# Some of the second weight parts made by GpSimd instead of VectorE, in two stretches of a two-block transformer kernel

## The chip, the cores and the metric

One core of one Trainium2 chip runs the whole program in one launch. The metric is the device time of one execution in microseconds (us), the lower the better; the median of several runs counts. The engines are named as the profile names them: PE (TensorE, matmuls; PEld is its weight load), DVE (VectorE), ACT (ScalarE), POOL (GpSimd), SP (the queue that issues the weight transfers).

## The reference, cut to what matters

Two transformer blocks follow each other on 256 tokens of width 1024, all in fp32. Block 1 has a mixer (an mLSTM of four heads beside a sliding-window attention of eight heads), a cross attention to 256 memory rows, and PEER: product keys choose 16 of 16384 experts for each token and head, of which each is one row of `expert_down` and one of `expert_up`. Block 2 has gated linear attention (GLA) beside MoBA attention, an MLP with squared ReLU, and a gated embedding. Shortened:

```
proj = rmsnorm(h, g_mix) @ w_in            # mq mk mv mo gates aq ak av
h = h + concat([mlstm(...), window(...)]) @ w_out
h = h + cross_attention(rmsnorm(h), rmsnorm(mem), ...)
h = h + peer_ffn(rmsnorm(h), ...)          # then a final norm
u = rms_norm(x, norm_mix_2) @ w_in_2       # gq gk gv lr gr mq mk mv gates
x = x + (sigmoid(ga)*gla(...) + sigmoid(gb)*moba(...)) @ w_out_2
x = x + square(relu(rms_norm(x) @ w_up_2)) @ w_down_2 ; x = x + gate*(p @ w_ple_2)
```

Every product of a weight with an activation is a dense matmul; PEER is computed over all experts with a gate that is zero for those not chosen.

## The kernel before, in words

Matmuls run in a rounded fp32 format, and each fp32 operand is split in two parts to keep its precision: `hi` is the value rounded, `lo` is the value less `hi`. A product is three matmuls: hi by hi, hi by lo, lo by hi (`mm3`, L339 to L341, where the weight is the stationary operand, and L378 to L380 in `unit_N`, where the activation is).

Weights come in 494 chunks of 128 x 1024 fp32 (512 KB), in the order of the list `ORDER`. The class `Stream` carries each through the same steps: SP issues the transfer into one of four `raw` tiles; ACT casts it to `hi` (L123, one of four tiles); DVE or POOL subtracts to get `lo` (L135, one of four tiles); PE uses both. `Stream.take(name)` is called by PE's code for each chunk c. It first issues the cast for all chunks up to c + 3 and the subtraction for all up to c + 2. Which engine subtracts is read from `PLAN`, a table from a chunk's name to a pattern that holds from that chunk on; the entry of the pattern is the chunk's number modulo the pattern's length. `AV` means cast on ACT and subtraction on DVE, `AG` means cast on ACT and subtraction on POOL:

```
self.pattern = self.plan.get(self.order[c][0], self.pattern)
first, second = self.pattern[c % len(self.pattern)]
...
(self.nc.vector if eng == "V" else self.nc.gpsimd).tensor_tensor(lo[:, o], raw[:, o], hi[:, o],
                                                                op=OP.subtract)
```

Everything else is written as chains: Python generators (`Chains`) that issue a few instructions at each tick. A tick comes after each unit of matmuls. So the order of the instructions of each engine is fixed when the program is built: it is the order in which takes, evacuations and ticks issue them, and each engine runs its own in that order.

The mixers' middle has the chunks mk0, mk1, mq0, mq1, mo0 to mo3 (numbers 11 to 18). Around them lie the chains `mem_chain` (splits and squares the memory: DVE L305, POOL adds L462 and L464), `mlstm` (a scan at L511, exponents from PSUM at L525 and L527, a POOL triangle mask at L532), the convolution in the evacuation of mk and mq (`ev_conv`, DVE L682 to L686), and `window` (DVE L636 to L642). The chunk after them is xk0.

Block 2 begins with bk0 to bk7, bq0 to bq7, lr0, gv4 to gv7 (numbers 331 to 351), each unit of four chunks in `unit_N`. The chain `norms` runs beside them: it adds up squares of the residual, on DVE (L1033, L1099) and POOL (L1034, L1100), sums them over partitions on PE (L1105), and gets 1/sqrt by `newton` (L286 to L300) on two numbers per partition, in some ten small DVE instructions. Evacuations of the units of block 2 are held until `norms` is done, as they need its scale: bk's are ACT L1388 and, per head, DVE L1286 (squares and their sum). Units of `unit_N` use two of five PSUM banks. The chain `setup` (POOL memsets L1273 to L1275), `keys` (L1256, L1262), `queries` and `stream` follow. The chunk after gv7 is gk0.

Of the kernel before, what the change touches and what calls it, by code (L numbers as in the profile page):

```python
# [52 lines left out]
for _name, _w in (("avg", 3), ("aq", 4), ("mk", 2), ("mq", 2), ("mv", 4), ("mo", 4), ("xk", 8), ("xv", 8),  # L53
# [18 lines left out]
          ("keys", 0): 1, ("keys", 1): 1, ("keys", 2): 3, ("keys", 3): 1, ("keys", 4): 2, ("queries", 1): 3,  # L72
          ("gla", 1): 1, ("gla", 8): 1, ("gla_out", 2): 1}

PLAN = {"mv0": ("AV",), "xo2": ("AG",), "down20": ("AV",), "down28": ("AG",), "down45": ("AV",),
        "upw0": ("AV", "AG"), "upw122": ("AV",), "up3": ("AV", "AG"), "up31": ("AV",)}


def chunks(s):
# [129 lines left out]
def block_kernel(ctx, tc, xT, memT, pT, wst, dwn, upw, keysT, gate_w2, cols, rows, out):  # L209
# [20 lines left out]

    ws.plan = PLAN
    ch = Chains()
# [1393 lines left out]
```

## Time and profile before

| | |
|---|---|
| time, median of 3 runs | 1566.12 us (1564.64 to 1566.81) |
| the profiled execution, its own time | 1564.55 us |
| its span, first to last instruction | 1562.8 us |
| busy: PE, PEld | 98%, 91% |
| busy: DVE, ACT, POOL | 73%, 51%, 27% |
| DMA | 169 GB/s read from HBM over the span |

The span is 1.75 us shorter than the execution's own time. Times in rows are us from the span's start. A row of the timeline gives start, duration, engine, line, operation, tiles and shapes, how many instructions are merged in it, and in brackets how long the engine had been idle before and what ended that.

### The profile page before, as it was taken

The numbers are of one execution on the slowest core, as the hardware profiler recorded it, in microseconds if no ns is written. First come the engines' busy times: TensorE is split into PE (matmuls) and PEld (weight loads), VectorE is DVE, ScalarE is ACT, GpSimd is POOL, SyncE is SP. The second block draws the span as 40 slices with busy tenths as digits, with TensorE's granted clock in tenths as the row PEclk, the third lists the DMA queues.
The fourth block names the chain that finished last, engine by engine and source line by source line (L and its number), as shares of the span: only waits on it lengthen the run. The fifth ranks groups of instructions, "written<-read, shape, count | busy, mean of one in ns | idle before, by whom it ended". The sixth has DMA issues, their size and how long they took to land.

```text
span 1562.8 us, 27506 instructions
## 1 busy us (share of the span) xinstructions
PE 1528.3 (98%) x10818; PEld 1417.9 (91%) x10818; DVE 1145.2 (73%) x2070; ACT 800.9 (51%) x1338; POOL 425.8 (27%) x238
## 2 busy tenths in 40 slices
PE   9899999999999999999999999999999999999998
PEld 8799999999999999998888888877888999999998
DVE  7977753877978899967777777759984656876456
ACT  7655553554445555454554554546654644544443
POOL 2210077645400000014444444403030000386000
PEclk9999999999999999999999999999999999999999
DMA  8335455455454444455656666645454365566553
GB/s 273 112 109 172 144 161 164 147 166 174 150 184 152 156 156 155 156 178 192 196 189 192 198 192 195 193 152 181 145 180 153 111 189 176 162 189 210 188 178 120
DMA packets 75713, 265.32 MB, mean 170 GB/s; under 512 B 8368, under 2 KB 11952, under 8 KB 75584
## 3 DMA queue, kind: packets, MB, share of 16 engines
q1 hardware_dynamic: 74848, 262.31, 52.9%
q8 instruction: 84, 1.38, 0.4%
q10 hardware_dynamic: 736, 1.27, 0.3%
q14 instruction: 45, 0.37, 0.1%
HBM read 262.49 MB, written 1.05 MB: 169 GB/s over the span
## 4 chain that ended last, share of the span: by engine, by line
PE 84%; DVE 13%; issue 1%; ACT 1%; DMA 1%; POOL 0%; SPq 0%; DVEq 0%; ACTq 0%; POOLq 0%
PE mm L339 16%; PE mm L341 16%; PE mm L340 16%; PE mm L1020 7%; PE mm L1018 7%; PE mm L1019 7%; DVE lo L135 3%; PE mm L380 2%; PE mm L379 2%; PE mm L378 2%; PE at L964 2%; DVE cb L877 1%; DVE cb L874 1%; DVE scr L1286 1%; DVE cb L876 1%
## 5 line engine op out<-in xcount | busy, mean ns | idle before, releaser
L123 ACT CAST hi<-raw 128x1024 fp32r<-128x1024 f32 (+1 forms) x495 | 517.0, 1046 | 290.1 <-issue 170.8
L135 POOL TENSOR_TENSOR lo<-raw,hi 128x1024 fp32r<-128x1024 f32 x134 | 325.3, 2428 | 738.6 <-ACT hi L123 736.5
L135 DVE TENSOR_TENSOR lo<-raw,hi 128x1024 fp32r<-128x1024 f32 (+1 forms) x361 | 447.7, 1250 | 25.4 <-ACT hi L123 25.1
L341 PE MATMUL mm<-XD,lo 128*128 128x256 f32 x1024 | 290.9, 284 | 6.7 <-DVE lo L135 6.7
L339 PE MATMUL mm<-XD,hi 128*128 128x256 f32 x1024 | 296.2, 289 | 0.0
L340 PE MATMUL mm<-XD,hi 128*128 128x256 f32 x1024 | 290.2, 283 | 0.0
L1003 DVE SCALAR_TENSOR_TENSOR ring<-cb,ring 128x256 fp32r<-128x256 f32 x128 | 172.0, 1345 | 94.0 <-ACT ring L1002 94.0
L341 PEld LDWEIGHTS mm<-XD,lo 128*128 128x128 f32 x1024 | 196.9, 192 | 7.9 <-DVE lo L135 7.9
L1018 PE MATMUL mm<-hi,ring 128*128 128x512 f32 x512 | 199.2, 389 | 1.0 <-DVE cb L984 1.0
L1020 PE MATMUL mm<-hi,ring 128*128 128x512 f32 x512 | 199.3, 389 | 0.0
L1019 PE MATMUL mm<-lo,ring 128*128 128x512 f32 x512 | 199.2, 389 | 0.0
L340 PEld LDWEIGHTS mm<-XD,hi 128*128 128x128 f32 x1024 | 197.1, 192 | 0.0
L339 PEld LDWEIGHTS mm<-XD,hi 128*128 128x128 f32 x1024 | 196.9, 192 | 0.0
L339 PE MATMUL mm<-XH,hi 128*128 128x256 f32 x584 | 168.6, 289 | 0.6 <-DVE hT L394 0.6
L341 PE MATMUL mm<-XH,lo 128*128 128x256 f32 x584 | 165.9, 284 | 0.6 <-DVE lo L135 0.6
L340 PE MATMUL mm<-XL,hi 128*128 128x256 f32 x584 | 165.8, 284 | 0.0
L1018 PEld LDWEIGHTS mm<-hi,ring 128*128 128x128 f32 x512 | 96.1, 188 | 21.0 <-ACT ring L1002 1.2
L339 PEld LDWEIGHTS mm<-XH,hi 128*128 128x128 f32 x584 | 112.6, 193 | 2.1 <-issue 1.5
L1020 PEld LDWEIGHTS mm<-hi,ring 128*128 128x128 f32 x512 | 96.1, 188 | 20.2 <-DVE ring L1003 0.4
L1019 PEld LDWEIGHTS mm<-lo,ring 128*128 128x128 f32 x512 | 96.1, 188 | 20.1
L341 PEld LDWEIGHTS mm<-XH,lo 128*128 128x128 f32 x584 | 112.6, 193 | 0.8 <-DVE lo L135 0.8
L340 PEld LDWEIGHTS mm<-XL,hi 128*128 128x128 f32 x584 | 112.6, 193 | 0.2
(464 smaller groups left out, 2963.5 us busy)
## 6 DMA issues: line engine op xcount, KB each, us to landing
raw<-in_wst SPq DMA_DIRECT2D x237, 512.0 KB, 3.7
raw<-in_dwn SPq DMA_DIRECT2D x128, 512.0 KB, 3.6
raw<-in_upw SPq DMA_DIRECT2D x128, 512.0 KB, 4.1
hT<-in_xT SPq DMA_DIRECT2D x4, 256.0 KB, 4.8
memt<-in_memT SPq DMA_DIRECT2D x1, 1024.0 KB, 6.1
out<-hT SPq DMA_DIRECT2D x7, 128.0 KB, 1.7
rowt<-in_rows ACTq DMA_DIRECT2D x1, 640.0 KB, 5.9
raw<-in_wst SPq DMA_DIRECT2D x2, 256.0 KB, 3.5
```

What stands on the lines that cost most here:

```text
L123: self.nc.scalar.copy(hi[:, o], raw[:, o])
L135: (self.nc.vector if eng == "V" else self.nc.gpsimd).tensor_tensor(lo[:, o], raw[:, o], hi[:, o], op=OP.subtract)
L339: T.matmul(ps, lhsT=wh, rhs=xh, start=start, stop=False)
L340: T.matmul(ps, lhsT=wh, rhs=xl, start=False, stop=False)
L341: T.matmul(ps, lhsT=wl, rhs=xh, start=False, stop=stop)
L378: T.matmul(pss[tb], lhsT=xh, rhs=h, start=kd == 0, stop=False)
L379: T.matmul(pss[tb], lhsT=xh, rhs=l, start=False, stop=False)
L380: T.matmul(pss[tb], lhsT=xl, rhs=h, start=False, stop=kd == 7)
L1003: V.scalar_tensor_tensor(lo, cb[:, j], 1.0 / GATE, hi, op0=OP.mult, op1=OP.subtract)
L1018: T.matmul(o, lhsT=ch, rhs=wh, start=j == 0, stop=False)
L1019: T.matmul(o, lhsT=ch, rhs=wl, start=False, stop=False)
L1020: T.matmul(o, lhsT=cl, rhs=wh, start=False, stop=j == 127)
```

## The change

Four entries are added to `PLAN`. The first pair makes the pattern ("AV", "AG") hold from mk0 up to xk0, the second from bk2 up to gk0.

```diff
-PLAN = {"mv0": ("AV",), "xo2": ("AG",), "down20": ("AV",), "down28": ("AG",), "down45": ("AV",),
-        "upw0": ("AV", "AG"), "upw122": ("AV",), "up3": ("AV", "AG"), "up31": ("AV",)}
+PLAN = {"mv0": ("AV",), "mk0": ("AV", "AG"), "xk0": ("AV",), "xo2": ("AG",), "down20": ("AV",), "down28": ("AG",), "down45": ("AV",),
+        "upw0": ("AV", "AG"), "upw122": ("AV",), "bk2": ("AV", "AG"), "gk0": ("AV",), "up3": ("AV", "AG"), "up31": ("AV",)}
```

By the chunk numbers the odd ones move: mk0, mq0, mo0, mo2 (11, 13, 15, 17) in the mixers, and bk2, bk4, bk6, bq0, bq2, bq4, bq6, lr0, gv5, gv7 (333 to 351) in block 2. For these 14 chunks the subtraction at L135 is issued on POOL instead of DVE, at the same place of the program; the casts, the transfers and the matmuls are issued as before.

## Rows read from the trace of the kernel before

**Rows 1.** Page, part 1: busy us, share of the span, instructions of each engine.
```profile
PE 1528.3 (98%) x10818; PEld 1417.9 (91%) x10818; DVE 1145.2 (73%) x2070; ACT 800.9 (51%) x1338; POOL 425.8 (27%) x238
```

**Rows 2.** Waits of PE, 28 to 77 us: total us, times, longest.
```profile
PE mm L379 <- DVE lo L135: 4.0, 4, 2.1
```

**Rows 3.** Waits of PE, 1049 to 1122 us.
```profile
PE mm L379 <- DVE lo L135: 2.5, 4, 0.8
```

**Rows 4.** Windows: stretch, length, busy us of each engine (instructions), clock, DMA.
```profile
45.00:60.00 15.00, 14.07 (x95) 11.82 (x94) 14.57 (x31) 6.00 (x7) 3.74 (x4) 1.00 0.27 95
60.00:77.00 17.00, 13.37 (x62) 9.69 (x62) 16.41 (x49) 13.90 (x29) 1.26 (x2) 1.00 0.41 116
...
1060.00:1078.00 18.00, 16.75 (x76) 13.48 (x77) 17.59 (x32) 12.62 (x20) 9.69 (x9) 1.00 0.52 176
1078.00:1100.00 22.00, 20.27 (x91) 15.96 (x90) 20.51 (x86) 9.12 (x12) 2.60 (x4) 1.00 0.56 178
```

**Rows 5.** Page, part 5: the subtraction on each engine, busy us, mean ns.
```profile
L135 POOL TENSOR_TENSOR lo<-raw,hi 128x1024 fp32r<-128x1024 f32 x134 | 325.3, 2428 | 738.6 <-ACT hi L123 736.5
L135 DVE TENSOR_TENSOR lo<-raw,hi 128x1024 fp32r<-128x1024 f32 (+1 forms) x361 | 447.7, 1250 | 25.4 <-ACT hi L123 25.1
```

**Rows 6.** Timeline of DVE in the expert-up stage.
```profile
1002.56 2.41 DVE L1003 SCALAR_TENSOR_TENSOR ring<-cb,ring 128x256 fp32r<-128x256 f32 x1 [1.03 <-ACT ring L1002]
1005.28 0.42 DVE L1003 SCALAR_TENSOR_TENSOR ring<-cb,ring 128x256 fp32r<-128x256 f32 x1 [0.31 <-ACT ring L1002]
```

**Rows 7.** Timeline of POOL, same stretch.
```profile
1002.30 2.40 POOL L135 TENSOR_TENSOR lo<-raw,hi 128x1024 fp32r<-128x1024 f32 x1 [3.04 <-ACT hi L123]
```

**Rows 8.** Timeline of ACT in the mixers: the cast of mk0.
```profile
32.72 1.03 ACT L123 CAST hi<-raw 128x1024 fp32r<-128x1024 f32 x1
```

**Rows 9.** Timeline of DVE in the mixers.
```profile
34.75 0.88 DVE L305 SCALAR_TENSOR_TENSOR meml<-memt,colt,memh 128x256 fp32r<-128x256 f32 x2 [0.27 <-ACT memh L304]
...
43.62 0.92 DVE L684 TENSOR_SCALAR m<-n,colt 128x256 f32<-128x256 f32 x1
44.58 1.53 DVE L686 SCALAR_TENSOR_TENSOR m<-n,colt,m 128x256 f32<-128x256 f32 x3
...
58.10 0.55 DVE L636 SCALAR_TENSOR_TENSOR sA<-at,maskA 128x384 f32<-128x384 f32 x1
```

**Rows 10.** Timeline of POOL in the mixers.
```profile
42.33 2.06 POOL L462 TENSOR_TENSOR memt<-memt 128x512 f32<-128x512 f32 x1 [0.74 <-ACT memt L460]
48.83 1.73 POOL L462 TENSOR_TENSOR memt<-memt 128x512 f32<-128x512 f32 x1 [4.44 <-ACT memt L460]
```

**Rows 11.** Timeline of POOL at the start of block 2.
```profile
1064.07 5.51 POOL L1034 TENSOR_TENSOR cb<-cb 128x512 f32<-128x512 f32 x3 [43.05 <-ACT cb L1096]
1069.66 1.60 POOL L1100 TENSOR_TENSOR cb<-cb 128x256 f32<-128x256 f32 x1
1072.16 0.95 POOL L1273 MEMSET rst<- 128x1024 f32 x1 [0.90 <-POOL cb L1100]
```

**Rows 12.** Timeline of DVE at the start of block 2.
```profile
1066.11 6.24 DVE L135 TENSOR_TENSOR lo<-raw,hi 128x1024 fp32r<-128x1024 f32 x3
...
1073.17 1.02 DVE L288 TENSOR_SCALAR rr<-nwi 128x2 int32<-128x2 int32 x1
```

**Rows 13.** Timeline of PE: bk6's second matmul, and bq0 going on after a wait.
```profile
1068.50 0.47 PE L379 MATMUL mm<-lo,XH 128*128 128x512 f32 x1
...
1076.66 0.50 PE L378 MATMUL mm<-hi,XH 128*128 128x512 f32 x1 [1.04 <-ACT kn L1388]
```

**Rows 14.** Timeline of DVE before the product keys, beside POOL's parts.
```profile
232.11 2.23 DVE L286 TENSOR_SCALAR nwi<-nwm 128x2 int32<-128x2 int32 x1
```

**Rows 15.** Timeline of PE, same place.
```profile
240.52 0.87 PE L321 MATMUL at<-cb,ones 128*128 128x128 f32 x4 [2.78 <-DVE cb L334]
```

**Rows 16.** Windows, columns as in rows 4: a stretch of low clock.
```profile
240.95:244.34 3.39, 3.39 (x18) 3.39 (x17) 1.42 (x4) 1.32 (x2) 1.52 (x1) 0.50 0.29 112
```

**Rows 17.** Groups of DVE instructions, 1078 to 1100 us, columns as in rows 5.
```profile
L1286 DVE SCALAR_TENSOR_TENSOR scr<-kn 128x128 f32<-128x128 f32 x16 | 4.7, 292 | 0.7
```

## The prediction

> **What bounds the kernel now.** The page comes first: PE is busy for 98% of the span, DVE for 73%, POOL for 27% [rows 1]. PE waits for little on the whole, so the change can win only what PE waits for in its two stretches, and can lose as much as it makes PE wait. The list of PE's waits, cut to each stretch, says how much there is to win: in the mixers PE waits four times for a second part made by DVE, 4.0 us together, in block 2's start four times, 2.5 us [rows 2, 3]. The table of windows says why: DVE is busy 14.57 of 15 us and 16.41 of 17 in the mixers, 17.59 of 18 and 20.51 of 22 in block 2 [rows 4]. There DVE sets the pace, and PE waits at the chunks whose subtraction stands far back in DVE's queue. So the question is not whether POOL has time (it is busy 1 to 10 us in these windows) but whether DVE gets time back, and whether POOL delivers in time.
>
> **What a moved part costs.** The groups by line give 1.25 us for the subtraction on DVE and 2.43 on POOL [rows 5]. Fourteen are moved, so 14 x 1.25 = 17.5 us of DVE work go and 34 us of POOL work come. But the two engines do not run freely beside each other. Lay the timelines of both over each other in the expert-up stage: one L1003 takes 0.42 us with POOL idle, and 2.41 us when it begins 0.26 us after a POOL subtraction of 2.40; it ends 0.27 us after that one's end [rows 6, 7]. DVE, which runs its queue in order, stood still; in that stage every second L1003 does. A tiny L286 before the product keys stands 2.23 us in the same way [rows 14]. What stands is an instruction with two inputs in SBUF, or one that reads SBUF alone like L286, or L684 with 0.92 us beside a POOL add [rows 9, 10]. L636, which reads PSUM and one SBUF tile, takes 0.55 us [rows 9]; such ones and max-reductions I take to pass.
>
> So a moved part gives DVE 1.2 us and takes up to 2.4, by what stands at the head of DVE's queue while POOL works. Where the head is of the standing kind that is a loss of up to 2.4 - 1.2 = 1.2 us for each.
>
> **The mixers, four parts.** I follow DVE's queue with this rule. *mk0:* its cast ends at 33.75 [rows 8], so POOL works until 36.2; L305, at 34.75 the next with two inputs [rows 9], stands for 1.45 us. With 1.2 us gone behind it that is +0.2. *mq0:* POOL makes it behind its first add L462 and ahead of the one at 42.33 [rows 10], until about 44.5. L684 comes 1.2 us earlier and ends no earlier than now, at 44.54 [rows 9]; the add, moved behind the part, now falls on the first L686, 1.5 us. Together +1.4. *mo0:* it comes behind the add of 48.83 [rows 10], and a small add follows it: three POOL instructions in a row under the next convolution's L684 and L686, +2.3, less 1.2 is +1.1. *mo2:* it falls on L636 and reductions [rows 9], which pass: +0.3, less 1.2 is -0.9. The sum is 0.2 + 1.4 + 1.1 - 0.9 = +1.8 us on DVE. The longest of PE's waits, 2.1 us, is for mo3's part [rows 2], which DVE still makes behind all this, so PE ends the stretch 1.8 us later. Bounds: -4.0, all of PE's waits [rows 2], to 4 x 1.2 = +4.8.
>
> **Block 2, the order of POOL's queue.** This is the largest term, and it is not about DVE's load. POOL has work of its own here: three adds L1034 from 1064.07 to 1069.58 and one L1100 to 1071.26, the first of which waits for ACT's squares [rows 11]. They are issued at the tick behind bk3's matmuls. bk6's subtraction is issued by the take of bk4, right behind this tick; on DVE it is the first of the three at 1066.11 [rows 12], behind L1033 and L1099 of the same tick. On POOL it comes behind all four adds: it begins at 1071.3 and ends 2.4 us later, at 1073.7, or 1.1 us later still if DVE's part of bk7 gets in between. PE wants it at 1068.50 [rows 13], and behind this matmul stands everything that PE has to do: 5.2 to 6.3 us of new wait, of which I take 5.5. The lower bound has the adds undisturbed, 1.73 us each [rows 10] and half of that for L1100: 1070.1, and 1072.5 with the part, +4.0. bk2 and bk4 are made before the adds, while DVE waits for ACT and PE: 0. bq0's part, next on POOL, ends 2.4 us behind bk6's, two chunks ahead of its use: 0. A raw tile is held until its subtraction is done, so bk6's lateness also delays the transfer into its tile, which is bq2's; PE is as late by then.
>
> **Clock.** Behind a wait of 2.78 us before the product keys [rows 15] PE runs 3.4 us at a granted share of 0.50, its lower level of 1.2 GHz [rows 16]; the trace has two more such stretches ahead of its end. A wait of 5.5 us should bring one: half of 3.4, +1.7. Bounds 0 and two stretches, 3.4.
>
> **The scale of `norms`.** PE's L1105, behind bk6, releases `newton`, and bq0 cannot go on before bk's evacuation L1388 has the scale; PE already waits 1.04 us for it [rows 13]. bk6's delay moves this whole chain and costs nothing twice. New is that bq2's part, cast when bk6's matmuls are over, falls on `newton`: one stand of some 2.0 us, against 0.9 us now (L288, 1.02 us beside POOL's memsets [rows 11, 12]): +1.1. The memsets move behind bq2's part, onto the rest of `newton`; the rows show an instruction of one SBUF input standing beside them and none of two, so I add nothing. Bounds 0, and 3.1 if every step stands beside the memsets, 2.0 us.
>
> The Trainium skill ("SBUF — State Buffer", section "Who interferes with whom") says that a two-input VectorE instruction collides with a GpSimd instruction that reads SBUF, and not with one that only writes it. By this rule the memsets hold none of the two-input steps and the sum stays as below; without it the sum would be 2.0 us more. The row of L288 agrees as far as it goes.
>
> **Block 2, the busy stretch.** From 1078 to 1100 us DVE does little but L1286 (two SBUF inputs, 0.29 us each [rows 17]), scales of the same kind, and subtractions. bq4, bq6 and lr0 are made beside them; each takes 2.4 and gives 1.2: +3.6 us. Of this PE's freed wait at bq6, no more than 0.8 [rows 3], and a little room at bq7 take 0.9: +2.7. gv5 and gv7 cost DVE as much, but none of PE's waits for parts is there: 0. Bounds: -2.5, all of PE's waits [rows 3], to +3.6.
>
> **Sum.** 1.8 + 5.5 + 1.7 + 1.1 + 2.7 = 12.8 us. On the profiled execution's own time, 1564.55 us (span 1562.8), that gives 1577.4; the median of the runs, 1566.12, is 1.6 higher and gives 1578.9. I say 1578. Nothing later takes it back: PE is busy throughout, and its later waits are for other things.
>
> **Rivals.** (1) *The lateness of bk6 alone.* Enough of DVE's instructions pass that it loses nothing on balance: mixers 0, busy stretch 0, scale 0; 5.5 + 1.7 = 7.2, 1573. For it: L636 passes; against: L1003 and L286 stand for nearly all of a part. (2) *Faster.* POOL's parts cost DVE nothing, and PE's waits for parts vanish: -4.0 - 2.5 = -6.5, 1560. Its place is mo1, mo3, bq3 and bq5; it decides if DVE's two-input instructions keep their length beside POOL, and bk6's part is there before 1068.5. Against it: rows 6 and 11. (3) *Nothing.* A part is issued two chunks ahead of its use and is ready in time wherever it is made: 1566. Against it: PE waits for eight parts now. (4) *Worse.* Two stretches of slow clock and all terms at their upper bounds: 4.8 + 6.3 + 3.4 + 3.1 + 3.6 = 21.2, 1587.
>
> The Trainium skill ("Perfetto Trace Analysis", section "Optimizing Scalar/DVE Operations") says that with VectorE saturated, handing work to another engine, even GpSimd, may make sense, which would be rival 2, and adds that these two share a read port, so that it might not help. The rows of L1003 agree with the second half.
>
> **How the numbers follow.** The forecast (1574 to 1583) has 0.62, rival 1 (1569.5 to 1574) 0.15, worse (beyond 1583) 0.13, nothing 0.06, faster 0.04. A difference under 0.2%, 3.1 us, is about what a measurement of this kernel cannot tell from no change. Forecast, rival 1 and worse are slower by more: 0.90; same 0.06; faster 0.04. For 8 in 10 the range takes in the forecast, most of rival 1 and the lower part of worse: 1570 to 1585.
>
> **What would show it.** Right: bk6's part on POOL begins behind L1100, PE waits over 4 us for it at its second matmul, with a stretch at 0.50 behind; L684, L686 and L1286 stand for up to 2.4 us beside POOL's parts; PE's wait for mo3 is as long or longer. Wrong: bk6's part is there before PE wants it, or L1286 keeps 0.29 us while POOL subtracts. If POOL takes bk6's part ahead of the adds, the largest term is gone and the sign is open.

## The result, and the profile after

The changed kernel takes 1577.86 us (median of 4 runs, 1576.46 to 1579.96), beside 1566.13 for the kernel before on the same chip: 1.008 times as long, 95% interval 1.0064 to 1.0095, or 11.7 us. The forecast was 1578, 1570 to 1585, and slower.

The profiled execution took 1579.96 us (span 1578.3). Page, parts 1 and 5, as in [rows 1, 5]:

```profile
PE 1537.0 (97%) x10818; PEld 1424.8 (90%) x10818; DVE 1148.3 (73%) x2056; ACT 801.4 (51%) x1338; POOL 459.1 (29%) x252
...
L135 POOL TENSOR_TENSOR lo<-raw,hi 128x1024 fp32r<-128x1024 f32 x148 | 360.7, 2438 | 818.0 <-ACT hi L123 802.9
L135 DVE TENSOR_TENSOR lo<-raw,hi 128x1024 fp32r<-128x1024 f32 (+1 forms) x347 | 429.3, 1246 | 26.5 <-ACT hi L123 26.3
```

Read the first row against the third. DVE lost 14 subtractions and 18.4 us in the group of L135, yet its busy time did not fall: it rose by 3.1 us. The work went away and the time stayed, in other instructions that took longer.

PE's waits in block 2's start, 1049 to 1135 us (total us, times, longest), to set beside [rows 3]:

```profile
PE mm L379 <- POOL lo L135: 4.3, 1, 4.3
PE mm L378 <- ACT kn L1388: 3.5, 1, 3.5
PE mm L379 <- DVE lo L135: 2.3, 3, 1.2
PE at L321 <- DVE dg L1128: 1.5, 1, 1.5
```

The waits for DVE's second parts, which the change could have won, are as long as before (2.3 against 2.5 us). Two new ones stand above them: bk6's part on POOL, and the scale of `norms`, which was 1.04 us [rows 13]. The mixers, 28 to 80 us, to set beside [rows 2]:

```profile
PE at L632 <- DVE sA L636: 2.2, 1, 2.2
PE mm L379 <- DVE lo L135: 0.7, 2, 0.4
```

There the wait for mo3's part did shrink, from 2.1 to 0.3 us (the 0.4 is mo1's), and one of the size it had for `window`'s L636 came ahead of it.

Where bk6's part was, on POOL's timeline (compare [rows 11]):

```profile
1060.81 2.85 POOL L135 TENSOR_TENSOR lo<-raw,hi 128x1024 fp32r<-128x1024 f32 x1 [3.30 <-ACT hi L123]
1065.30 4.70 POOL L1034 TENSOR_TENSOR cb<-cb 128x512 f32<-128x512 f32 x3 [1.65 <-ACT cb L1096]
1070.08 0.79 POOL L1100 TENSOR_TENSOR cb<-cb 128x256 f32<-128x256 f32 x1
1070.83 5.65 POOL L135 TENSOR_TENSOR lo<-raw,hi 128x1024 fp32r<-128x1024 f32 x2
```

The first row is bk4's part. The last holds bk6's and bq0's: bk6's begins when L1100 ends. On PE's timeline bk6's first matmul, its second behind the wait, bk7's first, bq0 going on behind its wait, and bq1's first:

```profile
1069.51 0.39 PE L378 MATMUL mm<-hi,XH 128*128 128x512 f32 x1
...
1074.20 0.50 PE L379 MATMUL mm<-lo,XH 128*128 128x512 f32 x1 [4.30 <-POOL lo L135]
...
1079.23 0.48 PE L378 MATMUL mm<-hi,XH 128*128 128x512 f32 x1
...
1086.38 0.79 PE L378 MATMUL mm<-hi,XH 128*128 128x512 f32 x1 [3.46 <-ACT kn L1388]
...
1090.39 0.63 PE L378 MATMUL mm<-hi,XH 128*128 128x512 f32 x1
```

From such first matmuls comes the table that the experiments are read by. Each entry is the start of a chunk's first matmul less that of an earlier chunk's, in us; labels are those of the experiments below.

| PE's time between first matmuls of | before | after | e2 | e3 | e4 | e5 | e8 | e11 |
|---|---|---|---|---|---|---|---|---|
| bk6 and bk7 | 3.63 | 9.72 | 9.71 | 7.49 | 10.25 | 4.00 | 3.67 | 7.51 |
| bk7 and bq1 | 6.95 | 11.16 | 9.78 | 9.26 | 6.92 | 13.18 | 7.70 | 6.93 |
| bq1 and lr0 | 23.54 | 25.37 | 25.93 | 27.26 | 23.54 | 25.72 | 27.44 | 23.56 |
| lr0 and gv7 | 17.18 | 18.92 | 18.92 | 20.39 | 17.19 | 18.93 | 18.92 | 17.19 |

The loss of the profiled execution is 6.1 + 4.2 + 1.8 + 1.7 = 13.9 us here, and the mixers add 0.7 (PE begins xk0 1.4 us later than before, of which 0.66 stood ahead of them). With the 0.66 us by which the two traces already differ ahead of the mixers, this is the 15.4 us between the two profiled executions; the medians are 11.7 apart, so this execution is one of the longer ones.

What DVE did at bk4 and at the scale of `norms`:

```profile
1062.70 2.04 DVE L135 TENSOR_TENSOR lo<-raw,hi 128x1024 fp32r<-128x1024 f32 x1 [1.31 <-ACT hi L123]
1064.66 4.19 DVE L1033 TENSOR_TENSOR cb<-cb 128x512 f32<-128x512 f32 x3
...
1079.92 3.28 DVE L286 TENSOR_SCALAR nwi<-nwm 128x2 int32<-128x2 int32 x1
1082.22 0.98 DVE L287 TENSOR_SCALAR nwh<-nwm 128x2 f32<-128x2 f32 x1
1083.23 1.02 DVE L288 TENSOR_SCALAR rr<-nwi 128x2 int32<-128x2 int32 x1
```

bk5's part took 2.04 us instead of 1.2 beside bk4's on POOL, so L1033 came later and fell on POOL's adds: 4.19 us. L286, two numbers per partition, stood for 3.28: POOL's part of bq2 ran from 1079.88 to 1082.28 and a memset from 1082.22 to 1083.17. L287 ended in the same moment as L286, at 1083.20, so only L288 comes on top, with the 1.02 us that it took before [rows 12]. The groups of L1286, 1085 to 1110 us, as [rows 17]:

```profile
L1286 DVE SCALAR_TENSOR_TENSOR scr<-kn 128x128 f32<-128x128 f32 x16 | 6.7, 421 | 0.7
L1286 DVE SCALAR_TENSOR_TENSOR scr<-qn 128x128 f32<-128x128 f32 x8 | 4.4, 555 | 0.3
```

421 and 555 ns are means over instructions that passed in 0.29 us and a few that stood for a whole part: 16 x (0.421 - 0.292) = 2.1 us in the first group. DVE in the mixers (compare [rows 9]), each time with POOL's part in the same microseconds except the last:

```profile
43.45 1.96 DVE L684 TENSOR_SCALAR m<-n,colt 128x256 f32<-128x256 f32 x1
45.44 2.44 DVE L686 SCALAR_TENSOR_TENSOR m<-n,colt,m 128x256 f32<-128x256 f32 x3
...
52.51 3.90 DVE L686 SCALAR_TENSOR_TENSOR m<-n,colt,m 128x256 f32<-128x256 f32 x3
...
60.23 0.55 DVE L636 SCALAR_TENSOR_TENSOR sA<-at,maskA 128x384 f32<-128x384 f32 x1
```

Windows, columns as in [rows 4]: the mixers, block 2's start, and two stretches behind the two waits.

```profile
45.00:60.00 15.00, 13.66 (x98) 12.10 (x96) 14.61 (x26) 4.87 (x6) 7.26 (x7) 1.00 0.34 106
60.00:77.00 17.00, 15.43 (x58) 10.89 (x59) 16.41 (x50) 13.72 (x29) 3.12 (x3) 0.80 0.30 96
1060.00:1078.00 18.00, 12.89 (x50) 9.88 (x49) 10.54 (x8) 9.87 (x16) 13.79 (x7) 0.92 0.45 150
1078.00:1100.00 22.00, 18.54 (x73) 14.85 (x72) 19.44 (x67) 8.75 (x11) 8.72 (x6) 0.83 0.49 157
...
1075.04:1078.45 3.41, 3.41 (x11) 2.67 (x9) 0.00 (x0) 0.00 (x0) 1.44 (x1) 0.50 0.95 330
1085.28:1092.10 6.82, 5.72 (x14) 4.46 (x15) 6.12 (x36) 3.47 (x5) 0.30 (x1) 0.50 0.27 82
```

In the mixers DVE is as busy as it was (14.61 and 16.41 us, 14.57 and 16.41 before), with fewer subtractions in it. Behind each of the two long waits PE runs at 0.50, the lower level of 1.2 GHz. The second such stretch ends at 1092.10, after bq1's first matmul: half of the 1.71 us between them, some 0.9, is in the table's 1.8 us from bq1 to lr0. The 0.80 of the window from 60 to 77 us is a stretch at half clock too; e2's profile has one in the same place (63.38 to 66.79 us), though its mixers are those of before.

### The profile page after: what moved, and what is told of

Read it like the earlier page. It is cut to its first block, busy times and chain, and to the rows that moved or that the text cites. A ratio compares the mean times of both kernels' runs of the same rounds, so it can differ in the third digit from the quotient of the medians.

```text
span 1578.3 us, 27512 instructions
## 1 busy us (share of the span) xinstructions
PE 1537.0 (97%) x10818; PEld 1424.8 (90%) x10818; DVE 1148.3 (73%) x2056; ACT 801.4 (51%) x1338; POOL 459.1 (29%) x252
## 4 chain that ended last, share of the span: by engine, by line
PE 82%; DVE 13%; ACT 1%; issue 1%; DMA 1%; POOL 1%; SPq 0%; DVEq 0%; ACTq 0%; POOLq 0%
PE mm L339 16%; PE mm L341 16%; PE mm L340 16%; PE mm L1018 7%; PE mm L1020 7%; PE mm L1019 7%; PE mm L379 2%; PE mm L380 2%; PE mm L378 2%; PE at L964 2%; DVE lo L135 2%; DVE scr L1286 1%; DVE cb L877 1%; DVE cb L874 1%; DVE m L686 1%
## 5 line engine op out<-in xcount | busy, mean ns | idle before, releaser
L135 POOL TENSOR_TENSOR lo<-raw,hi 128x1024 fp32r<-128x1024 f32 x148 | 360.7, 2438 | 818.0 <-ACT hi L123 802.9
L135 DVE TENSOR_TENSOR lo<-raw,hi 128x1024 fp32r<-128x1024 f32 (+1 forms) x347 | 429.3, 1246 | 26.5 <-ACT hi L123 26.3
```

## The experiments

Each ratio is against the kernel before, run on the same chip in the same rounds, with its 95% interval; microseconds are the ratio times that kernel's median. Where a diff shows one entry of `PLAN`, the rest of the kernel is the one before.

**The two halves.** e1 has only the mixers' entries, e2 only block 2's.

```diff
e1: +"mk0": ("AV", "AG"), "xk0": ("AV",),
e2: +"bk2": ("AV", "AG"), "gk0": ("AV",),
```

> Only the mixers' four parts (mk0, mq0, mo0, mo2) go to GpSimd. Theory of the held VectorE queue: +0.5 to +2 us against the kernel before; the trace of the full change shows PE only 0.7 us later behind the mixers, so I lean to the lower end. Rival, that VectorE time is freed: -2 to -4 us, PE's waits for parts gone.

> Only block 2's ten parts go to GpSimd. Theory: nearly the whole loss is here, +10 to +13 us, with a wait of 4 us for bk6's part and slow clock behind. Rival, that both stretches lose alike by VectorE's load (4 parts against 10): +8 us here and +3 in the mixers.

e1: 0.9999 [0.9985, 1.0013], no change that can be told. e2: 1.0074 [1.0054, 1.0094], +11.6 us. The whole loss is block 2's. In e1's trace PE is 0.7 us late at xk0, with the same exchange as after: mo3's wait gone, 2.2 us at L632 in its place.

**bk6's part in POOL's queue.** e4 moves bk6 alone, e3 all of block 2's parts but bk6.

```diff
e3: +"bk2": ("AV", "AG"), "bk6": ("AV",), "bq0": ("AV", "AG"), "gk0": ("AV",),
e4: +"bk6": ("AG",), "bk7": ("AV",),
```

> Block 2's parts as in the run before, but bk6's stays on VectorE. Theory of GpSimd's queue order: 6 us less than with all ten, so +5 to +7 us against before, no wait for a GpSimd part. Rival, that the loss is VectorE's held queue alone: within 1.5 us of the run with all ten, as one part in ten hardly changes it.

> bk6's part alone goes to GpSimd. Theory of the queue order: +5 to +7 us (a wait of 4 to 5 us at bk6's second matmul and a stretch of half clock behind it). Rival, load alone: -1 to +1 us.

e4: 1.0049 [1.0032, 1.0067], +7.7 us for one part of 494. POOL's timeline, PE's wait and a window of e4:

```profile
1063.53 5.48 POOL L1034 TENSOR_TENSOR cb<-cb 128x512 f32<-128x512 f32 x3 [43.06 <-ACT cb L1096]
1069.09 1.59 POOL L1100 TENSOR_TENSOR cb<-cb 128x256 f32<-128x256 f32 x1
1070.63 2.33 POOL L135 TENSOR_TENSOR lo<-raw,hi 128x1024 fp32r<-128x1024 f32 x1
```
```profile
PE mm L379 <- POOL lo L135: 4.9, 1, 4.9
```
```profile
1072.96:1076.37 3.41, 3.35 (x8) 2.68 (x9) 0.00 (x0) 0.00 (x0) 0.01 (x1) 0.50 0.69 210
```

In the table, e4 loses 10.25 - 3.63 = 6.6 us at bk6 and nothing anywhere else: 4.9 of wait and, in the half-speed stretch, 1.7. Here the part is the only thing moved, and DVE's load has no share in it.

e3, without bk6, is still 1.0054 [1.0035, 1.0073], +8.4 us: 3 less than e2, where 6 less was expected. PE waited 2.1 us at the same matmul, now for DVE. That called for e11.

**bk2 and bk4.** e11 moves these two alone, the step that the prediction gave 0.

```diff
e11: +"bk2": ("AV", "AG"), "bk6": ("AV",),
```

> bk2's and bk4's parts alone on GpSimd. The prediction costs them at nothing. The trace of the run without bk6 shows another way: bk4's part holds back bk5's on VectorE by 0.8 us, VectorE's three L1033 then meet GpSimd's three adds and take 4.2 us in place of 2.1, and bk6's part comes 2 us late: +2 to +4 us. By the prediction's step: 0.

e11: 1.0031 [1.0016, 1.0045], +4.9 us. L1033 of `norms` on DVE's timeline, in the kernel before, and then in e11 with bk5's part ahead of it:

```profile
1062.61 2.14 DVE L1033 TENSOR_TENSOR cb<-cb 128x512 f32<-128x512 f32 x3
```
```profile
1059.62 2.04 DVE L135 TENSOR_TENSOR lo<-raw,hi 128x1024 fp32r<-128x1024 f32 x1 [1.30 <-ACT hi L123]
1061.58 4.19 DVE L1033 TENSOR_TENSOR cb<-cb 128x512 f32<-128x512 f32 x3
```

bk4's part on POOL holds bk5's on DVE by 0.8 us. In the kernel before L1033 is through 0.7 us after POOL's adds begin [rows 11]; starting that much later, it runs beside them and takes twice as long. bk6's part, behind it on DVE, is ready 2.1 us after PE wants it; with the slow stretch behind the wait PE loses 7.51 - 3.63 = 3.9 us.

**Getting bk6's part ahead of the adds.** e5 is the changed kernel with one line: the tick of `norms` issues the waiting subtraction before its own adds.

```diff
             yield 2
+            ws.second_upto(ws.cut)
             for n in range(8):
```

> All fourteen parts on GpSimd as in the change, but bk6's part is issued ahead of the four adds of the norm instead of behind them; engines and work are the same. Theory of the queue order: PE's wait of 4.3 us for bk6 and its slow clock go, so about 6 us less than the change, +4 to +7 against before. Rival, that the loss at bk6 comes from GpSimd's slowness or from the held port: the wait stays over 3 us and the time within 1.5 us of the change.

e5: 1.0062 [1.004, 1.0085], +9.7 us, 2 less than the change where 6 less was expected. PE's wait for bk6 is gone (0.15 us left) and bk6 takes 4.00 us in the table. But the wait came back two chunks later, in bq0. PE's waits and DVE's timeline of e5:

```profile
PE mm L378 <- ACT kn L1389: 5.2, 1, 5.2
```
```profile
1073.61 2.10 DVE L1112 SCALAR_TENSOR_TENSOR nwm<-m,nwm 128x2 f32<-128x2 f32 x1
1075.74 3.19 DVE L286 TENSOR_SCALAR nwi<-nwm 128x2 int32<-128x2 int32 x1
```

The adds on POOL now end later, with bq0's and bq2's parts behind them, and the little chain that makes the scale stands through both parts: L1112 for the end of one, L286 for the other and a memset. So here that chain decides when PE goes on, after a wait of 5.2 us.

**bq2's part alone.** e6 moves only the part that falls on that chain.

```diff
e6: +"bq2": ("AG",), "bq3": ("AV",),
```

> bq2's part alone on GpSimd, where it falls on the newton steps of the norm. Theory of the held instruction: one of these steps stands over 2 us, PE's wait for bk's evacuation at bq0 grows from 1.0 to 2 to 3 us, +1 to +2 us in all. Rival, that tiny instructions slip past: the wait stays at 1.0 us and the time does not change.

e6: 0.9999 [0.9985, 1.0013]. The first two L298 of the chain took 2.50 us in its trace instead of 0.48, and PE's wait for the scale went from 1.0 to 1.8 us. But e8's trace has the same 1.8 with bq2's part on DVE and no step standing longer than before, so the 0.8 is not shown to be the part's; the times resolve nothing here.

**The busy stretch.** e8 moves bq4, bq6, lr0, gv5 and gv7 alone.

```diff
e8: +"bq4": ("AV", "AG"), "gk0": ("AV",),
```

> Only bq4, bq6, lr0, gv5 and gv7 on GpSimd, in the stretch where VectorE does little but two-input steps. Theory: L1286 and its like stand for over 2 us beside each, and PE comes out +2 to +4 us later, the waits for bq5's and bq7's parts longer. Rival, that relief of VectorE outweighs: -1 to -2.5 us.

e8: 1.0029 [1.0017, 1.0042], +4.5 us. In the table +3.9 between bq1 and lr0 and +1.7 behind lr0. The second is a stretch of slow clock, in gv6, that the kernel before does not have. Windows of e8, of the kernel before in gv6, and of e1, in which nothing of block 2 is moved:

```profile
1121.61:1125.02 3.41, 3.41 (x11) 2.64 (x10) 3.38 (x7) 3.22 (x4) 0.00 (x0) 0.50 0.01 2
```
```profile
1116.75:1119.58 2.83, 2.83 (x15) 2.34 (x14) 2.79 (x7) 2.54 (x3) 0.00 (x0) 1.00 0.03 13
```
```profile
1115.15:1121.98 6.83, 6.25 (x17) 4.59 (x17) 5.49 (x12) 3.78 (x4) 0.00 (x0) 0.50 0.22 70
```

All five profiles with gv5 moved (after, e2, e3, e5, e8) have it between 1121 and 1134 us, and the table has 1.7 us or more in them. Of those without, before, e4, e6, e7, e11 and e12 have none there. But e1 has one in the same place, and so has e10 below, with no part moved (1115.36 to 1118.77 us): lr0 to gv7 takes 20.00 and 18.71 us there, 2.8 and 1.5 more than before. So the stretch comes more often with gv5 moved, and that the move brings it is not shown.

**What holds DVE: a second reader, or any work on POOL?** e9 and e10 leave all parts on DVE and only add work to POOL at the same five chunks, into a tile that nothing reads. e9 adds the subtraction itself, a second time; e10 adds a subtraction of one column, which waits for the same cast, and then 2.5 us of memsets.

```diff
                                                                                 op=OP.subtract)
+e9:         if self.order[c][0] in ("bq4", "bq6", "lr0", "gv5", "gv7"):
+                self.nc.gpsimd.tensor_tensor(self.junk, raw, hi, op=OP.subtract)
+e10:        if self.order[c][0] in ("bq4", "bq6", "lr0", "gv5", "gv7"):
+                self.nc.gpsimd.tensor_tensor(self.junk[:, 0:1], raw[:, 0:1], hi[:, 0:1], op=OP.subtract)
+                for _ in range(2):
+                    self.nc.gpsimd.memset(self.junk, 0.0)
+                self.nc.gpsimd.memset(self.junk[:, 0:512], 0.0)
             self.parts[c] = (hi, lo)
...
+both:   ws.junk = wk.tile([128, 1024], FT, name="junk")
```

> The kernel before, with all parts on VectorE, and GpSimd makes the parts of bq4, bq6, lr0, gv5 and gv7 a second time into a tile that nobody reads. No matmul waits for GpSimd. Theory of the held VectorE: five holds of 2.4 us without the 1.2 us each that moving gives back, so worse than moving the same five (+0.29%): +6 to +11 us. Rival, that the loss there is GpSimd's parts coming late: 0 to +1 us, as VectorE's parts are still there.

> The same, but at each of the five places GpSimd fills the unread tile with zeros for 2.4 us after a one-column step that waits for the cast, so it is as busy and reads nothing. Theory, that what collides is GpSimd's reading with a second input of VectorE: 0 to +1 us, only one-input steps stand. Rival, that any work on GpSimd holds VectorE: +6 to +11 us as with the reading run.

e9: 1.0094 [1.0076, 1.0113], +14.7 us, more than the 6 to 11 expected. DVE keeps its five parts here, so nothing is given back for what stands; that was in the expectation. What was not is the clock. In its profile PE's waits for second parts and for `gl` grew from 2.5 + 1.2 to 6.3 + 4.8 us, and besides PE ran at half clock in three stretches between 1086 and 1132 us, 17.1 us together, where the kernel before has none. The longest:

```profile
1121.08:1131.32 10.24, 7.11 (x17) 4.88 (x18) 7.21 (x14) 2.73 (x3) 0.00 (x0) 0.50 0.34 104
```

e10: 1.0015 [1.0004, 1.0026], +2.3 us. Its profile has two half-speed stretches in block 2's start, 3.41 us each, and the runs don't tell how much is theirs and how much that of the one-input steps below. Groups of DVE instructions, 1074 to 1115 us, in e9 and then in e10, and of e10 a one-input step with POOL's memsets beside it:

```profile
L1289 DVE SCALAR_TENSOR_TENSOR scr<-qn 128x128 f32<-128x128 f32 x16 | 8.3, 517 | 1.1 <-ACT qn L1391 0.5
L1289 DVE SCALAR_TENSOR_TENSOR scr<-kn 128x128 f32<-128x128 f32 x16 | 6.7, 422 | 0.7
```
```profile
L1292 DVE SCALAR_TENSOR_TENSOR scr<-kn 128x128 f32<-128x128 f32 x16 | 4.7, 292 | 0.7
L1292 DVE SCALAR_TENSOR_TENSOR scr<-qn 128x128 f32<-128x128 f32 x16 | 4.6, 290 | 0.6
```
```profile
1085.00 0.98 DVE L291 TENSOR_SCALAR nwi<-nwm 128x16 int32<-128x16 int32 x1
1083.99 1.97 POOL L140 MEMSET junk<- 128x1024 f32 x2
```

With five subtractions the squares of L1286 stand as after the change; with memsets of the same length they keep their 0.29 us. So it is not POOL being at work that holds them, but what it does. The step of `newton` on 128 x 16 (L286 before the added lines) is the other kind: with one input it takes 0.98 us beside memsets, and 0.17 the second time, with POOL idle.

**The mixers: can the wait for mo3 be won?** e7 moves mo3's part, the one that PE waits 2.1 us for. e12 does the same but holds it on POOL, by a copy of one column that waits for `norm_chain`, until DVE has only L636 and reductions before it.

```diff
e7: +"mo3": ("AG",), "xk0": ("AV",),
e12, with e7's entry:
+            if self.order[c][0] == "mo3":
+                self.nc.gpsimd.tensor_copy(self.junk, self.after)
             lo = self.split.tile([128, 1024], FR, tag="lo", name="lo")
...
             V.tensor_scalar(dg[:, tb], ident, nat[:, tb:tb + 1], None, op0=OP.mult)
+        ws.after = dg[:, 1, 0:1]
```

> mo3's part alone on GpSimd. It would work from about 57.5 to 60 us of the old trace, where VectorE has L636 and reductions, which read PSUM or one tile. Theory (what counts is what stands at the head of VectorE's queue): nothing stands, PE's wait of 2.1 us at mo3 goes, -1 to -2 us. Rival, that every part on GpSimd costs VectorE over a microsecond net: 0 to +1.5 us.

> mo3's part alone on GpSimd, as in the earlier run, but GpSimd first waits, by a one-column copy, for the last step in front of the next L636 of VectorE, so that the part falls on L636 and reductions and not on L686. Theory (the head of VectorE's queue decides): no stand, PE's waits at mo3 go to under 1 us, -1 to -2 us. Rival, that GpSimd's parts never pay in this stretch: 0 to +1 us.

e7: 1.0008 [0.9996, 1.0021]; e12: 1.0002 [0.9991, 1.0012]. Neither gains. DVE's timelines of e7 and of e12 (lines 4 higher), with POOL's part from 57.93 to 60.32 in the first and 68.88 to 71.25 in the second:

```profile
56.86 3.74 DVE L686 SCALAR_TENSOR_TENSOR m<-n,colt,m 128x256 f32<-128x256 f32 x3
```
```profile
68.58 0.55 DVE L640 SCALAR_TENSOR_TENSOR sA<-at,maskA 128x384 f32<-128x384 f32 x1
69.17 0.61 DVE L642 TENSOR_REDUCE mxA<-sA 128x1 f32<-128x128 f32 x2
...
70.93 0.34 DVE L644 TENSOR_TENSOR mxA<-mxA,rowt 128x4 f32<-128x4 f32 x1
```

In e7 the part fell on the convolution, which was not where it was expected; PE lost the wait for mo3 and got one of 2.4 us at L632. In e12 nothing of DVE's stood for long, and the second parts cost PE 1.9 + 0.8 = 2.7 us of waits for DVE and POOL instead of 4.0 [rows 2]. That 1.3 us is 0.1% and lies within the interval.

## Why the prediction was right, and where it was not

The sign and the two main mechanisms were right, and so was the total; two of its zeros were not, one term was too small, and slow clock came in more places than the one it was counted for. That 1577.86 lies 0.14 us from 1578 is luck: terms that were missing or too small stood against others that were too large or hid behind one another, and single executions lie 1.4 below to 2.1 above the median.

- *A moved part gives 1.2 us and takes up to 2.4.* Shown: DVE's busy time in the profile of after did not fall, L686, L684, L1286 and L286 stood, and in e12 L636 and reductions passed beside a part. e9 against e10 shows that for two-input instructions it takes a POOL instruction that reads. The Trainium skill's rule ("SBUF — State Buffer", section "Who interferes with whom"), that a two-input VectorE instruction does not collide with a GpSimd instruction that only writes, agrees: 0.29 us beside memsets in e10, 0.42 and 0.52 on average beside subtractions in e9. The row of L288 that the prediction set beside it has one input and tests nothing of this.
- *bk6's part behind POOL's four adds*, 5.5 us of wait and 1.7 of slow clock. Shown by e4: 4.9 and 1.7. In the changed kernel the wait was 4.3 and the slow clock 1.8. POOL's adds were shorter there than in [rows 11] (4.70 and 0.79 us, beside L1033 and no longer beside three subtractions), and bk6's part longer, from 1070.83 until PE goes on at 1074.20: bk7's part on DVE got in between, as the prediction had left open.
- *bk2 and bk4: 0.* Wrong; +4.9 us by themselves (e11). The step looked at whether these two parts would be ready, and not at what they run beside: bk5's part and then, through its lateness, L1033. That is the prediction's own rule of two inputs, not applied to this place.
- *These two terms don't add.* Alone, bk2 with bk4 and bk6 lose 3.9 and 6.6 us on PE by the table; together 6.1. With bk6's part on POOL, PE waits for POOL's queue, and DVE's lateness is hidden behind that wait. So the wrong zero cost the total nothing. It cost e3 and e5 their expected gain: taking bk6's lateness away left another wait directly behind.
- *The scale of `norms`: +1.1.* Too small: the wait grew by 2.4 us in the profile of after (3.46 less 1.04), by 1.4 in e2's. L286 stood through the whole of bq2's part, 2.4 us, as it had 2.23 in [rows 14], and in the profile of after through the memset behind it too. The bound of 3.1 held. The claim that memsets hold none of the two-input steps is e10's result; that they cannot prolong the stand of a one-input step was assumed and is wrong. With bq2's part alone (e6) the wait was 0.8 longer at most; the rest needs bk6's lateness, behind which L286 begins together with bq2's part.
- *Clock: one stretch, +1.7.* Right behind bk6's wait, 1.8. Not counted was a second one behind the wait for the scale, which at 3.46 us was longer than the 2.78 that the term was taken from: of the 4.2 us from bk7 to bq1 it is 4.2 - 2.4 = 1.8 in the profile of after, and 2.8 - 1.4 = 1.4 in e2's. With the 0.9 behind bq1 the clock cost 4.5 us in the profile of after, over the bound of 3.4, and 3.2 in e2's.
- *The busy stretch: +2.7 between bq4 and lr0.* Right mechanism; by the table, from bq1 to lr0, +2.4 in e2, +3.9 alone (e8), and +1.8 in the profile of after, of which some 0.9 is the end of that slow stretch.
- *gv5 and gv7: 0.* The five profiles with these parts moved are 1.7 us or more longer here. PE's waits for `gl` are all but the same (1.3 us against 1.2), and the loss is a half-speed stretch. e1 and e10 have such a stretch without these parts moved, so whether the move is its cause stays open; what differs in the rows is 0.15 us more of PE standing behind gv5 and, in bq7, the wait of 1.5 us at L321 ahead of it.
- *The mixers: +1.8.* The instructions stood as followed through (mq0 on L684 and L686, mo0 on L686 with 3.90 us, mo2 on hardly anything), and the windows show DVE no freer. PE lost 0.7 us in two traces, and e1 no time that can be told, so the 1.8 is not borne out. PE's wait for mo3 did not stay "as long or longer", as the prediction said; it moved to L636, ahead of mo1, which waits in the same DVE queue, and PE came to mo3 3.2 us later.
- *Rivals.* "Faster" falls with e1, e7 and e12: even the part that PE waited longest for gave nothing measurable. "Lateness of bk6 alone" falls with e8, +4.5 us with bk6's part where it was; in e3, +8.4, bk6's part was late on DVE. "Worse" did not come, since the terms hid behind one another: moved alone, the five groups give 0 + 4.9 + 7.7 + 0 + 4.5 = 17.1 us, together 11.7 (bq0's part was not run alone, and each time is known to 2 to 3 us, so that this difference by itself is hardly clear of noise; the table shows the hiding at bk6).

## What to carry to other kernels

Before moving an elementwise step from VectorE to an idle GpSimd, lay both queues over each other for the time of the step: VectorE's two-input instructions beside a GpSimd subtraction stood here until it was done, and then 1.2 us given away cost up to 2.4. See also what stands ahead of the step in GpSimd's own queue, and when PE wants the result: one part behind four adds cost 7.7 us, more than all the waits that the change was after. Losses that sit one behind another on the same path are not to be added, and removing the first of them gives back only what the next leaves.

## What was not expected of the hardware

- An instruction that stands can stand again: L286, of 0.2 us, was held by POOL's part and then by the memset behind it, 3.28 us without a break. In e2 the same instruction got through between the two (2.38 us).
- Memsets on POOL hold one-input instructions of VectorE (0.98 us instead of 0.17 in e10) though the two-input ones pass them (0.29).
- Most stretches at half clock in these profiles are 3.41 or 6.82 us long, and each costs PE about half its length where PE is the bound. In code that no edit touched they come and go between executions (the profile of e1 has one of 6.8 us at 1115 us, which before has not and which makes gv5 to gv7 2.8 us longer), so two single profiles can differ by 2 to 3 us for that alone.
